# A two-layer diffusion backbone on one core: when the first map's row products are issued, and the order of the first input

## Chip, core and metric

The kernel runs on one NeuronCore of one Trainium2 chip. The metric is device time in microseconds (us) of one execution of the whole program. Engines are called by their names: TensorE (PE, with its weight loads as PEld), VectorE (DVE), ScalarE (ACT), GpSimd (POOL) and SyncE (SP), whose queue issues nearly all DMAs.

## What is computed

Two layers act on 384 tokens (one prompt of 128, one sample of 256) of width 1024 in float32. Cut to what matters:

```python
def _layer(x, cond, lp, mixer_fn):
    mod = silu(cond) @ lp['w_ada'] + lp['b_ada']          # 1024 -> 6 * 1024
    sh1, sc1, g1, sh2, sc2, g2 = split(mod, 6)
    y = mixer_fn(x * (1 + sc1) + sh1)                      # four mixers, four gates, w_o
    x = layernorm(ALPHA * x + g1 * y)
    f = square(relu((x * (1 + sc2) + sh2) @ lp['w_up'])) @ lp['w_down']
    return layernorm(ALPHA * x + g2 * f)
```

The mixer projects its input onto the queries, keys and values of four mixers (A latent attention, B two-way retention, C windowed attention, D grouped attention) and onto four gates, multiplies each mixer's output by a branch matrix and its gate, adds the four and applies `w_o`. There are two conditions (prompt and sample), so `mod` is two vectors of 6144 per layer. "The first map" is `w_ada`: it turns the condition into shifts, scales and gates.

## The kernel before

**Precision.** Each large product is made of three TensorE products of float32r halves: `mm3` (lines 119 to 122) multiplies high by high, high by low and low by high. A weight tile comes by DMA into one of six raw buffers of 128x1024 (`raw_load`, line 270). ScalarE casts it to its high half (line 281) and VectorE subtracts that for the low half (`split_low`, line 125). `Stream` (line 238) does this for all weights in the order of use: it loads four ahead and splits two ahead.

**The order of work.** Instructions are written in program order, and a scheduler then orders each engine's own by priority and readiness. Where the order matters the kernel pins it: `in_order` (line 156) keeps what is written inside it in written order on the engines named, `held` (line 145) keeps instructions behind given earlier ones of the same engine, and `keep` fixes single ones.

**The first input** (lines 473 to 561, layer 0 only). The shift and scale of the first modulation are needed before anything else. For each of eight groups k of 128 channels, `first_part(k)` makes the first map's product on TensorE: condition as weights, 16 products that leave four partial sums on four groups of partitions (line 330), copied out by ScalarE (line 333). `first_input(k)` transposes them (line 339), reduces the four partials on VectorE (line 341), adds the bias (line 343), adds one to the scale (line 495) and makes the modulated channels: ScalarE the high half (line 499), VectorE the full value (line 500) and the low half. `split_w(i)` splits the weights of two of the projection's column groups, `w_qa` (416 columns, mixer A) and `w_c0` (512 columns, mixer C). `chunk` (line 516) then adds one channel group's products into three banks (one per 128 tokens) of either. Four products with zeros stand ahead of it all (`WARM`, line 544). Only TensorE is kept in written order here.

**Attention.** The remaining projections come as `chunks` (line 1088), 256 columns at a time, through two PSUM banks (`psg`); the banks of mixers C and A are first evacuated by ScalarE (line 597, called in lines 1089 to 1095). Beside them runs `Pipe` (line 416): a list of tasks, each a list of stages; every `tick()` (line 464) starts one task and advances each live one by one stage. Layer 0 has 16 ticks in the projections (22 in layer 1) and then two per pair of gate products (`gates`, line 1109), eight per branch, in the order A, C, D, B. In `attend`, `scores` computes a score tile, its maximum, the exponentials and their sum, and scales the tile by the reciprocal (line 671); `turn`, a tick later, transposes it; `values` multiplies by the values. `at` is the pool of the attention; `t2` in it has ten tiles of 128x512. Behind the third branch it is closed and the pool `p2` opened.

**The rest of the first map.** Only 8 of its 48 parts are made on TensorE. The others are row products on VectorE: `ada_vector` (line 346) loads 128 transposed rows of `w_ada` into a raw buffer (line 357, three loads ahead on SP's queue) and multiplies them by a condition's row with a running sum (line 370), one instruction for each of the two conditions. The rows of SiLU of the conditions are made by `cond_rows` (line 226): a 1 MB load, four tanh on ScalarE (line 231), eight operations on VectorE (lines 232 and 233). Layer 0's attention makes 48 row products (its own first gate, and the modulation of its MLP), layer 1's makes 32; the MLPs make the rest. `tick` calls them by `TICK_OPS` a tick once the tick's number is over `TICKS_FROM`:

```python
            if ticks[0] > TICKS_FROM:          # 22
                for _ in range(TICK_OPS[l]):   # 3 in layer 0, 2 in layer 1
                    next(ada_v, None)
```

What is not done by then is drained where the attention's pool is closed (line 1159).

**Layer norms.** `out_product` (line 1274) ends with a written order over three blocks of tokens (lines 1316 to 1376): `sums`, `normalise` (ScalarE, two halves of 512, line 1219), `turn` (eight transposes in two banks, line 1227, with the modulation behind them), `high` (ScalarE's cast, line 1244) and `low` (VectorE's subtraction, line 125), mixed with the next product's parts (`following`, lines 610 and 614).

Of the kernel before, what the change touches and what calls it, by code (L numbers as in the profile page):

```python
# [16 lines left out]
P = 128  # L17
D = 1024
KT = D // P
NTOK = 384  # L20
# [20 lines left out]
TICK_OPS = (3, 2)  # L41
TICKS_FROM = 22
# [6 lines left out]
WARM = 4  # L49
# [44 lines left out]
def kernel(ctx, tc, a):  # L94
# [363 lines left out]
    for l in range(L):  # L458
        last = l == L - 1
        pipe = Pipe()  # L460
        ada_v = ada_vector(AV_GATES[l], lambda: t2("acc"))
        ticks = [0]

        def tick():
            pipe.step()
            ticks[0] += 1
            if ticks[0] > TICKS_FROM:
                for _ in range(TICK_OPS[l]):
                    next(ada_v, None)


        if l == 0:
            with tc.tile_pool(name="start", bufs=1, reuse_waits="tile") as st:
# [12 lines left out]
                def load_w(i):  # L486
                    raws[i] = [raw_load(a["w_qa"][0, i]), raw_load(a["w_c0"][i])]
# [16 lines left out]
                def split_w(i):  # L504
                    if i == 0:

                        wh, wl = (q[:, :2 * A_W] for q in o_pair())
                        for c in (slice(0, A_W), slice(A_W, 2 * A_W)):
                            nc.scalar.copy(wh[:, c], raws[i][0][:, c])
                            split_low(wl[:, c], raws[i][0][:, c], wh[:, c])  # L510
                        w_a.extend(by_k([(wh, wl)], 2))
                    else:
                        w_a.extend(by_k([split_raw(raws[i][0], o_pair)], 2))
                    w_c.extend(by_k([split_raw(raws[i][1], ring_hl)], 2))
# [26 lines left out]
                with in_order((mybir.EngineType.PE,)):  # L541
                    idle = bank(psm)
                    for _ in range(WARM):
                        mm(idle[:, 0:256], lhsT=zero[:, 0:P], rhs=zero, start=True, stop=True)
                    first_part(0)
                    first_input(0)
                    split_w(0)
                    banks_a = [bank(psa) for _ in range(3)]
                    banks_c = [bank(pso), bank(psg), bank(psg)]
                    for k in range(0, KT, 2):  # L550
# [8 lines left out]
                        else:  # L559
                            chunk(banks_c, w_c, 512, k + 1)  # L560
# [12 lines left out]
        if l == 0:  # L573
            smalls = small_loads(0)
            cond_rows(lambda: t2("acc"))
# [48 lines left out]
        def attend(i, q_of, k_of, v_of, scale, sink=None, mask=None):  # L624
            ob = {}

            def batch(g, us):
# [9 lines left out]
                def scores():  # L637
# [31 lines left out]
                    for i, (u, nb, c) in enumerate(segs):  # L669
                        for j in range(2):  # L670
                            nc.vector.tensor_scalar(out=p[:, j, c], in0=p[:, j, c], scalar1=su[:, i, j:j + 1],
                                                    scalar2=None, op0=ALU.mult)
# [421 lines left out]
        for t in range(3):  # L1094
            evac_to("a", 0)(t, banks_a[t], A_W)
        for key, c0, scale in chunks:
# [35 lines left out]
        p2 = None  # L1132
# [531 lines left out]
```

## Time and profile before

| what | us |
|---|---|
| median of 3 runs | 1293.54 (1293.39 to 1294.13) |
| the profiled execution | 1292.02 |
| its span, first to last instruction | 1290.3 |
| TensorE busy / weight loads busy | 1258.5 / 1139.1 |
| VectorE busy | 865.3 |
| ScalarE busy | 567.0 |
| GpSimd busy | 198.9 |

Busy time is the time in which an engine executes; register, branch, semaphore and DMA-issuing instructions don't count. Matmuls are pipelined and their ends are modelled, so the busy time of TensorE says where it waited, and not that it ran at its peak. PEclk is the clock granted to TensorE as a share of 2.4 GHz; 0.50 is 1.2 GHz. In the views, L125 is line 125 of the kernel, and "tile<-tile" are the names of what is written and read.

### The profile page before, as it was taken

Reading aid. Unit: us, or ns where it says so; the run is one execution under the profiler, and the core shown is the slowest. Engines: PE = TensorE matmul, PEld = TensorE weight load, DVE = VectorE, ACT = ScalarE, POOL = GpSimd, SP = SyncE. Lnnn points to the kernel's source line nnn. Section 1 sums busy time; section 2 is a strip of 40 time slices with the busy share of each in tenths; the row PEclk is TensorE's granted clock in tenths of the full one; section 3 lists DMA queues with packets and bytes.
Section 4 is the critical chain, followed back from the end, with each engine's and each line's share of the span. In section 5 each row is a group of like instructions: output and inputs, shape, how many; then the busy total and the mean of one; then the engine's idle time right before and its main releaser. Section 6 shows DMA issues by size and latency. Waiting matters only on the chain. (4 is left out here: it accounts for less than half of the span.)

```text
span 1290.3 us, 19064 instructions
## 1 busy us (share of the span) xinstructions
PE 1258.5 (98%) x7226; PEld 1139.1 (88%) x7226; DVE 865.3 (67%) x1572; ACT 567.0 (44%) x1014; POOL 198.9 (15%) x214
## 2 busy tenths in 40 slices
PE   8999999979999999999999999999999999999996
PEld 5789888979989999999998988899998999999995
DVE  4655887998668999543384678799465893333336
ACT  4564453323536444454455455333343644444441
POOL 0011200423214000000051210023221500000003
PEclk9999999999999999999999999999999999999999
DMA  9832244559434888554314223447644263334421
GB/s 368 304 111 93 86 147 135 176 196 328 165 127 172 279 271 270 189 164 145 130 51 146 72 93 115 150 148 235 240 148 163 89 228 125 131 131 149 164 80 50
DMA packets 64684, 211.66 MB, mean 164 GB/s; under 512 B 9232, under 2 KB 13264, under 8 KB 64464
## 3 DMA queue, kind: packets, MB, share of 16 engines
q1 hardware_dynamic: 61872, 201.49, 44.9%
q0 software_dynamic: 2432, 8.42, 1.9%
q8 instruction: 57, 0.93, 0.3%
q10 hardware_dynamic: 288, 0.52, 0.1%
q14 instruction: 35, 0.29, 0.1%
HBM read 206.28 MB, written 4.13 MB: 163 GB/s over the span
## 5 line engine op out<-in xcount | busy, mean ns | idle before, releaser
L125 DVE TENSOR_TENSOR wl<-raw,wh 128x1024 fp32r<-128x1024 f32 x250 | 320.8, 1289 | 295.9 <-ACT wh L281 295.6
L281 ACT CAST wh<-raw 128x1024 fp32r<-128x1024 f32 x250 | 261.6, 1050 | 467.1 <-PE bank L121 309.2
L122 PE MATMUL bank<-hTh,wl 128*128 128x384 f32 x1040 | 350.0, 337 | 5.7 <-DVE wl L125 5.7
L120 PE MATMUL bank<-hTh,wh 128*128 128x384 f32 x1040 | 351.8, 338 | 0.6 <-ACT tt L1116 0.6
L121 PE MATMUL bank<-hTl,wh 128*128 128x384 f32 x1040 | 349.0, 336 | 0.0
L122 PEld LDWEIGHTS bank<-hTh,wl 128*128 128x128 f32 x1040 | 195.7, 188 | 7.1 <-DVE wl L125 6.9
L120 PEld LDWEIGHTS bank<-hTh,wh 128*128 128x128 f32 x1040 | 195.9, 188 | 5.8 <-issue 2.3
L121 PEld LDWEIGHTS bank<-hTl,wh 128*128 128x128 f32 x1040 | 195.7, 188 | 2.7 <-issue 0.5
L121 PE MATMUL bank<-wl,uh 128*128 128x512 f32 x384 | 150.4, 392 | 0.0
L122 PE MATMUL bank<-wh,ul 128*128 128x512 f32 x384 | 150.3, 392 | 0.0
L120 PE MATMUL bank<-wh,uh 128*128 128x512 f32 x384 | 149.7, 390 | 0.0
L370 DVE CUSTOM_DVE_ANT_0 acc<-raw,csr,bT 128x1024 bf16<-128x1024 f32 x80 | 103.6, 1321 | 0.0
L370 DVE CUSTOM_DVE_ANT_0 acc<-lnc,csr,bT 128x1024 bf16<-128x1024 f32 x80 | 100.5, 1292 | 0.0
L1143 POOL TENSOR_TENSOR tt<-tt,tt 128x384 f32<-128x384 f32 x48 | 64.4, 1361 | 214.1 <-DVE tt L1142 213.0
L122 PEld LDWEIGHTS bank<-wh,ul 128*128 128x128 f32 x384 | 71.9, 188 | 15.4 <-DVE ul L125 0.4
L120 PEld LDWEIGHTS bank<-wh,uh 128*128 128x128 f32 x384 | 72.1, 188 | 13.8
L121 PEld LDWEIGHTS bank<-wl,uh 128*128 128x128 f32 x384 | 72.1, 188 | 13.9
L120 PE MATMUL bank<-wh,hTh 128*128 128x256 f32 x240 | 72.2, 301 | 2.3 <-ACT tmc L597 2.3
L121 PE MATMUL bank<-wl,hTh 128*128 128x256 f32 x240 | 69.4, 289 | 0.0
L122 PE MATMUL bank<-wh,hTl 128*128 128x256 f32 x240 | 68.7, 286 | 0.0
L120 PEld LDWEIGHTS bank<-wh,hTh 128*128 128x128 f32 x240 | 46.5, 194 | 5.4 <-ACT tmc L597 2.6
L663 ACT ACTIVATE p<-bank,neg 128x384 f32<-128x384 f32 (+1 forms) x72 | 35.9, 509 | 33.7 <-DVE neg L660 19.5
(263 smaller groups left out, 1758.1 us busy)
## 6 DMA issues: line engine op xcount, KB each, us to landing
raw<-in_w_g_dram SPq DMA_DIRECT2D x64, 512.0 KB, 3.6
raw<-in_w_d_dram SPq DMA_DIRECT2D x64, 512.0 KB, 3.5
raw<-in_w_u_dram SPq DMA_DIRECT2D x58, 512.0 KB, 4.0
raw<-in_w_av_dram SPq DMA_DIRECT2D x40, 512.0 KB, 3.3
lnc<-in_w_av_dram SPq DMA_DIRECT2D x40, 512.0 KB, 4.3
raw<-in_w_q_dram SPq DMA_DIRECT2D x28, 512.0 KB, 4.4
raw<-in_w_ada_dram SPq DMA_DIRECT2D x16, 512.0 KB, 8.5
raw<-in_w_b_dram SPq DMA_DIRECT2D x16, 512.0 KB, 4.0
```

The source lines that it names most:

```text
L120: mm(out, lhsT=a_hl[0], rhs=b_hl[0], start=start, stop=False)
L121: mm(out, lhsT=a_hl[0], rhs=b_hl[1], start=False, stop=False)
L122: mm(out, lhsT=a_hl[1], rhs=b_hl[0], start=False, stop=stop)
L125: nc.vector.tensor_tensor(out=low, in0=x, in1=high.bitcast(F32), op=ALU.subtract)
L281: nc.scalar.copy(wh, raw)
L370: nc.vector.tensor_tensor_reduce(out=alloc().bitcast(BF16), in0=w, in1=csr[:, c], scale=1.0, scalar=bT[:, l, u, b:b + 1], op0=ALU.mult, op ...
L663: nc.scalar.activation(p[:, j, c], ss[j][:, c], AF.Exp, bias=neg[:, i, j:j + 1], scale=scale, accum_out=su[:, i, j:j + 1])
L1143: nc.gpsimd.tensor_tensor(out=acc[c], in0=acc[c], in1=t_, op=ALU.add)
```

## The change

It does six things. The row products of the attention are issued by a table of rates per two ticks: in both layers one per tick from tick 4, one per two ticks from tick 14, two per tick from tick 29; once `p2` is open, one per tick, with outputs in its `v2` tiles. The loop that drains them moves from the closing of the attention's pool to the place before the layer norm's constants. The rows of the conditions are made behind the first evacuations instead of ahead of them. The first channel group has a function of its own, `first_channels`: two products with a 0/1 matrix in place of the transposes and the reduction, the tokens of the prompt first, the first weights cast and split between, all four engines in written order, with zero products of 64 columns (three behind the first map's product, six behind the sums); the first weight load is cut in two, and two weights of the stream are split before the last chunk. One of the two scalings of each score tile goes from VectorE to ScalarE. The third block's normalisation is cut so that a cast comes between its halves.

```diff
-TICK_OPS = (3, 2)
-TICKS_FROM = 22
+TICK_OPS = ((4, 2), (14, 1), (29, 4))
-WARM = 4
+WARM = (4, 3, 6)
...
-        ada_v = ada_vector(AV_GATES[l], lambda: t2("acc"))
+        p2 = None
+        ada_v = ada_vector(AV_GATES[l], lambda: (v2 if p2 else t2)("acc"))
...
-            if ticks[0] > TICKS_FROM:
-                for _ in range(TICK_OPS[l]):
-                    next(ada_v, None)
+            n = 2 if p2 else ([0] + [c for f, c in TICK_OPS if f <= ticks[0]])[-1]
+            for _ in range((n + ticks[0] % 2) // 2):
+                next(ada_v, None)
...
                 def load_w(i):
-                    raws[i] = [raw_load(a["w_qa"][0, i]), raw_load(a["w_c0"][i])]
+                    first = raw_tile(2 * A_W)
+                    n = 2 if i == 0 else 1
+                    for c in (slice(j * 2 * A_W // n, (j + 1) * 2 * A_W // n) for j in range(n)):
+                        nc.sync.dma_start(out=first[:, c], in_=a["w_qa"][0, i][:, c])
+                    raws[i] = [first, raw_load(a["w_c0"][i])]
...
+                def first_channels():
+                    (ah, al), (ch, cl) = tuple(q[:, :2 * A_W] for q in o_pair()), ring_hl()
+                    ra, rc = raws[0]
+                    a0, a1, c0, c1 = slice(0, A_W), slice(A_W, 2 * A_W), slice(0, 512), slice(512, 1024)
+                    _, xk, part = inputs[0]
+                    mod = modT[0][:, 0]
+                    sel = st.tile([P, 2], F32, name="sel")
+                    nc.vector.tensor_reduce(out=sel, in_=ident.rearrange("p (j c) -> p c j", j=4)[:, 0:2, :], axis=AX.X,
+                                            op=ALU.add)
+                    pt = bank(psm)
+                    for b in range(2):
+                        mm(pt[:, 2 * b:2 * b + 2], lhsT=part[:, b * P:(b + 1) * P], rhs=sel, start=True, stop=True)
+                    warm_up(WARM[2])
+                    nc.scalar.copy(ah[:, a0], ra[:, a0])
+                    nc.vector.tensor_tensor(out=mod, in0=pt[:, 0:4].rearrange("p (b c) -> p b c", b=2),
+                                            in1=bT[:, 0, 0].unsqueeze(2).to_broadcast([P, 2, 2]), op=ALU.add)
+                    nc.vector.tensor_scalar(out=ms[:, 0], in0=mod[:, 1], scalar1=1.0, scalar2=None, op0=ALU.add)
+                    hx = st.tile([P, NTOK], F32, tag="hx", name=nm("hx"), bufs=2)
+                    for cnd, cs in ((0, slice(0, P)), (1, slice(P, NTOK))):
+                        m, sh = ms[:, 0, cnd:cnd + 1], mod[:, 0, cnd:cnd + 1]
+                        nc.scalar.activation(hT[0][:, 0, cs], xk[:, cs], AF.Identity, bias=sh, scale=m)
+                        if cnd == 0:
+                            split_low(al[:, a0], ra[:, a0], ah[:, a0])
+                        nc.vector.tensor_scalar(out=hx[:, cs], in0=xk[:, cs], scalar1=m, scalar2=sh, op0=ALU.mult,
+                                                op1=ALU.add)
+                    split_low(hT[1][:, 0, :], hx, hT[0][:, 0, :])
+                    for h, lo, r, c in ((ch, cl, rc, c0), (ah, al, ra, a1), (ch, cl, rc, c1)):
+                        nc.scalar.copy(h[:, c], r[:, c])
+                        split_low(lo[:, c], r[:, c], h[:, c])
...
-                with in_order((mybir.EngineType.PE,)):
-                    idle = bank(psm)
-                    for _ in range(WARM):
-                        mm(idle[:, 0:256], lhsT=zero[:, 0:P], rhs=zero, start=True, stop=True)
+                idle = bank(psg)
+                def warm_up(n, cols=64):
+                    for _ in range(n):
+                        mm(idle[:, 0:cols], lhsT=zero[:, 0:P], rhs=zero[:, 0:cols], start=True, stop=True)
+                with in_order():
+                    warm_up(WARM[0], 256)
                     first_part(0)
-                    first_input(0)
-                    split_w(0)
+                    warm_up(WARM[1])
+                    first_channels()
+                with held(last_issued()), in_order((mybir.EngineType.PE,)):
...
                         else:
+                            for i in range(SPLITS_AHEAD):
+                                stream.split(i)
                             chunk(banks_c, w_c, 512, k + 1)
...
             smalls = small_loads(0)
-            cond_rows(lambda: t2("acc"))
...
-                        for j in range(2):
-                            nc.vector.tensor_scalar(out=p[:, j, c], in0=p[:, j, c], scalar1=su[:, i, j:j + 1],
-                                                    scalar2=None, op0=ALU.mult)
+                        nc.scalar.mul(p[:, 0, c], p[:, 0, c], su[:, i, 0:1])
+                        nc.vector.tensor_scalar(out=p[:, 1, c], in0=p[:, 1, c], scalar1=su[:, i, 1:2], scalar2=None,
+                                                op0=ALU.mult)
...
             evac_to("a", 0)(t, banks_a[t], A_W)
+        if l == 0:
+            cond_rows(lambda: t2("acc"))
         for key, c0, scale in chunks:
...
-                    for _ in ada_v:
-                        pass
                     at_ctx.__exit__(None, None, None)
...
-            def normalise():
-                for h in range(2):
+            def normalise(hs=(0, 1)):
+                for h in hs:
...
-                normalise[2]()
+                normalise[2]((0,))
                 high[1](1)
+                normalise[2]((1,))
...
+        for _ in ada_v:
+            pass
         c1 = norm_consts(0)
```

## Rows read from the trace of the kernel before

**Rows 1.** The page, part 1: busy us, share of the span, instructions.
```profile
PE 1258.5 (98%) x7226; PEld 1139.1 (88%) x7226; DVE 865.3 (67%) x1572; ACT 567.0 (44%) x1014; POOL 198.9 (15%) x214
```

**Rows 2.** Busy us by stretch: PE, PEld, DVE, ACT, POOL (counts), PEclk, DMA share, GB/s.
```profile
12.00:15.30 3.30, 3.30 (x21) 1.50 (x20) 0.72 (x1) 0.36 (x1) 0.00 (x0) 0.50 1.01 398
56.40:59.70 3.30, 3.30 (x17) 3.30 (x17) 3.25 (x10) 1.23 (x4) 1.11 (x2) 0.50 0.40 112
278.20:281.50 3.30, 3.30 (x12) 3.30 (x11) 3.30 (x5) 0.66 (x1) 0.00 (x0) 0.50 0.82 278
60.00:226.00 166.00, 165.58 (x1128) 145.65 (x1128) 116.50 (x291) 81.64 (x199) 20.21 (x31) 1.00 0.34 116
226.00:306.00 80.00, 71.29 (x407) 67.92 (x405) 80.00 (x162) 22.23 (x35) 27.33 (x19) 0.98 0.59 202
306.00:356.00 50.00, 49.59 (x281) 48.82 (x282) 33.48 (x41) 23.62 (x34) 16.05 (x14) 1.00 0.67 243
770.00:850.00 80.00, 79.18 (x543) 70.65 (x542) 64.24 (x154) 35.12 (x81) 5.92 (x6) 1.00 0.37 126
850.00:900.00 50.00, 49.05 (x287) 48.38 (x286) 49.52 (x93) 16.46 (x25) 15.85 (x12) 1.00 0.63 206
```

**Rows 3.** Waits of TensorE, whole span: us in total, times, longest us.
```profile
PE bank L122 <- DVE wl L125: 7.1, 5, 3.0
PE bank L120 <- ACT tmc L597: 2.3, 1, 2.3
...
PE bank L120 <- DVE atts L981: 1.3, 2, 0.8
PE bank L1227 <- DVE hTl L125: 1.3, 3, 0.6
```

**Rows 4.** Timeline, first input: start us, us, instruction, [idle before it and releaser].
```profile
10.12 0.45 PE L523 MATMUL bank<-o,hTh 128*128 128x416 f32 x1 [2.11 <-ACT o L509]
...
12.91 1.94 PE L330 MATMUL bank<-raw,cs 128*32 128x256 f32 x16
```

**Rows 5.** Timeline around the first evacuations.
```profile
49.02 3.88 ACT L281 CAST wh<-raw 128x1024 fp32r<-128x1024 f32 x4
...
52.80 2.19 ACT L231 ACTIVATE acc<-csr 128x512 f32<-128x512 f32 x4
...
54.89 1.53 ACT L597 COPY tmc<-bank 128x512 f32<-128x512 f32 x3
...
55.51 0.39 PE L120 MATMUL bank<-wh,hTh 128*128 128x256 f32 x1 [2.30 <-ACT tmc L597]
```

**Rows 6.** Timeline around the longest wait for a weight split.
```profile
275.38 1.22 DVE L125 TENSOR_TENSOR wl<-raw,wh 128x1024 fp32r<-128x1024 f32 x1
...
276.65 0.44 PE L122 MATMUL bank<-hTh,wl 128*128 128x384 f32 x1 [3.05 <-DVE wl L125]
```

**Rows 7.** Costliest group of VectorE from 226 to 311 us: count, busy us, mean ns.
```profile
L370 DVE CUSTOM_DVE_ANT_0 acc<-raw,csr,bT 128x1024 bf16<-128x1024 f32 x35 | 45.8, 1337 | 0.0
```

**Rows 8.** Busy time of line 370 alone from 770 to 850 us.
```profile
770.00:850.00 80.00, 19.38 (x31) 1.00 0.37 126
```

**Rows 9.** Group of TensorE's products with 64 float32 columns.
```profile
L1007 PE MATMUL bank<-tmb,atts 128*128 128x64 f32 x64 | 7.6, 271 | 0.0
```

**Rows 10.** Timeline, third block of the first layer norm.
```profile
391.60 1.52 ACT L1219 ACTIVATE z<-z,lnrs 128x512 f32<-128x512 f32 x2 [0.37 <-POOL lnrs L1215]
...
393.03 0.56 ACT L1244 CAST hTh<-bank 128x512 fp32r<-128x512 f32 x1
...
394.37 0.66 PE L1227 MATMUL bank<-ident,z 128*128 128x128 f32 x4 [0.58 <-DVE hTl L125]
```

**Rows 11.** Groups of the wide scalings on VectorE and of ScalarE's line 777.
```profile
L671 DVE TENSOR_SCALAR p<-p,su 128x384 f32<-128x384 f32 x48 | 17.9, 415 | 0.5
...
L777 ACT ACTIVATE qA<-bank,rsa 128x384 f32<-128x384 f32 x6 | 3.5, 583 | 4.4 <-PE bank L772 4.4
```

**Rows 12.** Waits of all engines, whole span: us in total, times, longest us.
```profile
ACT wh L281 <- DMA raw<-in_w_g_dram: 24.3, 8, 4.9
```

More of the change, by code (lines that the diff above doesn't have):

```diff
@@ L504, in split_w @@
                 def split_w(i):
[L505 to L513, printed above, removed]
@@ L514, in split_w @@
-                    w_c.extend(by_k([split_raw(raws[i][1], ring_hl)], 2))
+                    w_a.extend(by_k([split_raw(raws[i][0], o_pair)], 2))
+                    w_c.extend(by_k([split_raw(raws[i][1], ring_hl)], 2))
+                def first_channels():
[27 more added lines that the diff above has]
+                        split_low(lo[:, c], r[:, c], h[:, c])
+                    w_a.extend(by_k([(ah, al)], 2))
+                    w_c.extend(by_k([(ch, cl)], 2))
@@ L1130, in products, with v2 @@
                 done(c0 + i, ts_[i], b[:, :NTOK])
-        p2 = None
+        def v2(name):
+            return p2.tile([P, 512], F32, tag="v2", name=nm(name), bufs=7)
         def T2(name, dt):
@@ L1183, in norm_consts @@
             return gb + [lnc(a[n][l]) for n in names]
-        def v2(name):
-            return p2.tile([P, 512], F32, tag="v2", name=nm(name), bufs=7)
         def layer_norm(t, banks, xt, consts, mod, final):
```

## Prediction

> **What bounds the kernel now.** I began with the shares of the span: TensorE is busy 1258.5 us of 1290.3, 98% [rows 1]. No gain is to be had from the totals of another engine; there are some 32 us of idle TensorE to win, and whatever it spends at the lower clock. The second view, busy time by stretch, says where [rows 2]. From 226 to 306 us TensorE is idle 80.00 - 71.29 = 8.7 us while VectorE is busy 80.00 of 80, and three short stretches (from 12.0, 56.4 and 278.2 us) show PEclk 0.50, that is 1.2 GHz instead of 2.4. The third view, what TensorE waited for, names causes [rows 3]: 7.1 us for VectorE's low weight halves (line 125, read by line 122), 2.3 us for ScalarE's first evacuation (line 597), 1.3 us for a low half of the normalised rows (line 125, read by line 1227). Each low-clock stretch comes behind one of TensorE's longest idles: 2.11 us before 10.12 [rows 4], 2.30 us before 55.51 [rows 5], 3.05 us before 276.65 [rows 6].
>
> The big one is VectorE between 226 and 311 us [rows 7]: 35 of the first layer's 48 row products (line 370) run there, 45.8 us or 1.31 us each. VectorE is in order, so a weight split sits behind row products: the one that starts at 275.38 lets TensorE go at 276.65, after its 3.05 us [rows 6].
>
> **The change, part by part.** The sum is made against the profiled execution, 1292.0 us; its span of 1290.3 has 1.7 us around it. The median of the runs is 1293.5, 1.5 above it, and I add that back at the end.
>
> *Row products spread.* Before, layer 0 issues 3 per tick from tick 23: 48 in ticks 23 to 38. So the loop that drains the rest behind tick 40 finds nothing, and removing it is worth nothing by itself. After: 10 in ticks 4 to 13, 7 in ticks 14 to 28, 24 in ticks 29 to 40, and the last 7 one per tick behind the attention. In the crowded stretch 24 stand where 35 ran: 11 x 1.31 = 14.4 us of VectorE's 85 go, so it falls from all of the time to some 83%. The nearest stretch with that load is 770 to 850, VectorE 64.24 of 80 (80%), where TensorE idles 0.82 us [rows 2]. I leave 0.9 us of the 8.7: gain 7.8. The idle before the low clock at 278.2 goes with it; 3.4 us at half rate cost 1.7. Together **9.5** (ends: half of it, 4.7, if VectorE still comes late to half of the splits; 10.4 if nothing is left). The seven behind the attention, 9.2 us, fall into 306 to 356, where VectorE is busy 33.48 of 50 [rows 2]: hidden, and if that cover is gone the last branch's splits come late by up to 1.31 us each, as in the lower end.
>
> *What the early ones cost.* 17 row products per layer now come at ticks 4 to 28, where in layer 0 VectorE is busy 116.50 of 166 and TensorE idles 166 - 165.58 = 0.4 us [rows 2]. An attention step queued behind one is late by at most 1.31 us, and its reader is a tick away. Below: nothing. Above: the wait on line 981's scores, 0.8 us at its longest [rows 3], stood in 770 to 850, which holds 19.38 us of row products [rows 8]; 34 of them, 44.5 us, give 44.5/19.38 x 0.8 = 1.8. Between the two: **-1.0**. Each also takes one of ten scratch tiles for its output, which nothing in the trace prices; it goes into the same bounds. Their rows of weights come through SP's one queue and the six raw buffers, three loads ahead, from tick 4 on: that is a rival below.
>
> *Layer 1.* 32 products, 2 per tick from tick 23 before; after, 17 before tick 29 and 15 in ticks 29 to 36. TensorE idles 0.82 + 0.95 = 1.8 us from 770 to 900 [rows 2]; I take half, having no row for a smaller load there: **1.0** (0 to 1.8).
>
> *Condition rows behind the evacuations.* Four tanh, 2.19 us, stand on ScalarE between the casts, which end at 52.90, and the first evacuation at 54.89; TensorE waits 2.30 us until 55.51 [rows 5]. After the move the first evacuation (1.53/3 = 0.51) ends near 53.4, TensorE was done at 53.2: 0.3 is left, 2.0 gained, and with it the low clock at 56.4 (1.7): **3.7**, ends 2.0 and 4.0. The two early weight splits are among the four casts already, so I count nothing for them. The tanh then hold up the evacuations behind them by 2.2 us at most, which the two output banks cover. On SP the load of the condition rows moves behind five small cache loads; its users are later too, so nothing.
>
> *First input.* Two products with a 0/1 matrix replace two transposes and a reduction, so one VectorE step of three before the rows' affine goes; the cast of the first weight half, which TensorE waits for at 10.12, leaves that path [rows 4]; the first token block alone lets TensorE start. Against that stand nine 64-column warm-up products ahead of the first real one: two records each, 7.6/64 = 0.12 us per record by the nearest kind [rows 9], so 0.7 us behind the first map's product and 1.4 behind the sums. TensorE then starts near 9.8 instead of 10.12 and reaches the second input's product, without the waits inside the first chunk, about 1 us before 12.91. That one took 1.94 us at the low clock [rows 4]. Its data had landed by 12.91 but need not be far ahead, so I credit 0.9 and 0.5 of what the clock costs: **1.4**. Ends: -0.6 if the warm-ups outlast the chain and the clock drops anyway; 2.9 if start and clock are both won in full. Cutting the first weight load in two adds one issue to SP's queue, hidden behind loads that wait for bytes.
>
> *The third block's normalisation in halves.* The cast at 393.03 moves ahead of the second half of line 1219 (1.52/2 = 0.76 us) and so does the split that frees the bank for the transposes at 394.37, which wait 0.58 [rows 10]. That half itself then ends later, near 393.7, and is the next to be late. There are three such turns, 1.3 us in all [rows 3]: **1.0** (0 to 1.3).
>
> *Half of the softmax scaling to ScalarE.* 36 of 72 scalings leave VectorE at 0.415 us for the wide ones and go to ScalarE, where the nearest row, line 777 with the same width and a scale per row, takes 0.583 [rows 11]. ScalarE is busy 81.64 of 166 there [rows 2], and the transposes that read the result come a tick later: nothing, either way; if that cover is gone, the price is the rival below. The Trainium skill's page "ScalarE: Activation LUTs", section "Rules for kernel authors", speaks against the edit: it puts a plain multiplication on VectorE and not on ScalarE. The rows agree that the single step is dearer there; whether that costs time hangs on the cover.
>
> Sum: 9.5 - 1.0 + 1.0 + 3.7 + 1.4 + 1.0 = 15.6 us, so 1276.4 by the profiled execution and **1278** as the median.
>
> **The rivals.** *VectorE stays the bound of the crowded stretch.* 24 products at two per tick still meet the splits and the retention steps there. For it: 83% is an average. Against it: the stretch at 80% with 0.82 us of idle. Half of the 9.5 stays and the early ones cost their 1.8: gain 15.6 - 4.8 - 0.8 = 10.0, 1283.5.
>
> *Raw buffers run short: slower.* With one product per tick or per two, three of six raw buffers are held from tick 4 to 47 instead of for 16 ticks, and on SP a weight load queues behind a row load that waits for its buffer. ScalarE's casts waited 24.3 us, 8 times, for such loads [rows 12], while TensorE lost 8.7 us in the crowded stretch. Were that so at ticks 4 to 28 of both layers, 2 x 8.7 = 17.4 us would come on top of the sum: 1295.5, and up to 1299 with two low-clock stretches. It decides from 15.6/47 = 0.33 us on each of the 47 weights used in those ticks. Against it: only eight casts in the whole span waited so, and slower use also asks for fewer bytes per tick.
>
> *The scalings on ScalarE come late.* If each of the 24 wide ones lay on the path, 24 x 0.583 = 14.0 us eat the sum: 1292, no change. Each transpose would have to catch up with a step issued a tick ahead.
>
> *The start and the moved rows do not do what they say*: the order on an engine is chosen by a scheduler, and casts or tanh may again come first. Then 3.7 and 1.4 go: gain 10.5, 1283.
>
> **How the numbers follow.** Forecast as worked out 0.61; VectorE still the bound 0.18; start and rows unmoved 0.06; scalings late 0.06; raw buffers short 0.09. About 0.2% (2.6 us) is what a measurement of this kernel can tell from no change. Faster by more: 0.61 + 0.18 + 0.06 = 0.85; the same 0.06; slower 0.09. The lower end takes the upper bounds together: 10.4 + 1.8 + 4.0 + 2.9 + 1.3 = 20.4, 1273. The upper end takes in the rivals at 1283 and 1283.5 with their own bounds, 1286; the 0.15 of the last two cases stays outside.
>
> **What would show it.** Right: no wait of TensorE over 1 us on line 125's work between 220 and 310 us, VectorE below 90% there, PEclk 1.00 around 56 and 278 us, the first product behind the input stage within 0.5 us of its forerunner, and TensorE's idle down by 10 us or more. Wrong: casts that wait for raw loads between 65 and 220 us, scalings as the releaser of transposes, or a new wait on VectorE before tick 28. If the crowded stretch keeps over 4 us of idle, the first term was mis-sized.

## The result, and the profile after

The changed kernel takes **1278.02 us** (median of 4 runs, 1276.57 to 1279.75) against 1293.47 us for the kernel before beside it (4 runs, 1290.49 to 1294.13): ratio 0.9886, 95% interval 0.9863 to 0.9908. That is 15.45 us less by the medians, where 15.6 were forecast. The profiled execution took 1276.65 us, its span is 1274.5.

The page after, part 1 (busy us, share of the span, instructions), to be held against [rows 1]:

```profile
PE 1253.8 (98%) x7246; PEld 1137.6 (89%) x7246; DVE 854.1 (67%) x1537; ACT 583.5 (46%) x1051; POOL 211.2 (17%) x214
```

TensorE's idle time went from 1290.3 - 1258.5 = 31.8 us to 20.7, by 11.1. The other 4.7 us of the span's gain are busy time, about what the three stretches at 1.2 GHz cost (3.41 us each at half rate, 5.1 in all). Busy time by stretch after, with the columns of [rows 2]:

```profile
12.00:15.30 3.30, 2.69 (x23) 1.61 (x20) 0.73 (x3) 0.37 (x1) 0.00 (x0) 1.00 1.03 401
56.40:59.70 3.30, 3.30 (x30) 3.30 (x29) 3.09 (x9) 1.94 (x7) 0.36 (x1) 1.00 0.89 330
278.20:281.50 3.30, 3.30 (x21) 3.30 (x20) 3.30 (x7) 1.55 (x2) 1.36 (x2) 1.00 0.85 281
60.00:226.00 166.00, 163.18 (x1107) 143.00 (x1106) 119.64 (x284) 89.98 (x213) 29.78 (x32) 1.00 0.36 121
226.00:306.00 80.00, 78.51 (x468) 77.69 (x467) 74.27 (x144) 24.48 (x36) 29.02 (x24) 1.00 0.60 205
306.00:356.00 50.00, 49.96 (x264) 46.48 (x263) 37.81 (x49) 23.45 (x34) 10.88 (x8) 1.00 0.73 261
770.00:850.00 80.00, 79.40 (x512) 72.78 (x511) 54.39 (x137) 32.71 (x70) 5.87 (x6) 1.00 0.33 112
850.00:900.00 50.00, 49.06 (x283) 48.45 (x282) 35.85 (x51) 17.78 (x25) 17.25 (x15) 1.00 0.71 256
```

All three stretches at 1.2 GHz are gone (PEclk 1.00 in the first three lines); in both kernels the only other such stretch lies behind the last product. Between 226 and 306 us TensorE idles 1.5 us instead of 8.7. VectorE, however, is still busy there for 74.27 of 80 us, 93%. The waits of TensorE over the whole span, with the columns of [rows 3]:

```profile
PE bank L1086 <- DVE oB L1078: 1.8, 2, 1.5
PE bank L718 <- ACT p L707: 1.5, 3, 0.8
PE bank L330 <- DMA raw<-in_w_ada_dram: 1.4, 3, 0.6
...
PE bank L122 <- DVE wl L125: 0.6, 1, 0.6
...
PE bank L120 <- ACT tmc L634: 0.2, 1, 0.2
```

The 7.1 us on low weight halves became 0.6, the 2.3 us on the first evacuation 0.2, and the wait of the transposes on the normalised rows' low half is no longer listed. Three small waits have moved to the top: the retention's normalisation on VectorE (line 1078; 0.9 us before), the score tiles scaled on ScalarE (line 707; 0.5 us before, on VectorE), and the loads of the first map's weights (0.4 us before).

Where the time came from is best read from instructions that both programs share. Each row gives an instruction's start in the two profiled executions; the last column, the worth of the stretch that ends there, is worked out from the differences.

| start of (us) | before | after | difference | of that stretch |
|---|---|---|---|---|
| last of the first map's products | 45.07 | 43.92 | -1.15 | first input -1.15 |
| first projection product behind the first evacuation | 55.51 | 52.28 | -3.23 | wait on the evacuation -2.08 |
| evacuation of the first gate product | 144.44 | 140.45 | -3.99 | low clock at 56.4, 11 of the 17 early row products: -0.76 |
| evacuation of the 17th gate product | 261.62 | 257.66 | -3.96 | the other 6 early row products: +0.03 |
| first turn of layer norm 1, layer 0 | 381.09 | 367.17 | -13.92 | crowded stretch **-9.96** |
| the same turn, layer 1 | 1004.98 | 989.81 | -15.17 | two turns -0.90, layer 1's attention -0.37 |
| last product | 1279.65 | 1263.97 | -15.67 | third turn -0.49 |

### The profile page after: what moved, and what is told of

Its sections match the earlier page's. It is cut to its first block, busy times and chain, and to the rows that moved or that the text cites. A ratio compares the mean times of both kernels' runs of the same rounds, so it can differ in the third digit from the quotient of the medians.

```text
span 1274.5 us, 19089 instructions
## 1 busy us (share of the span) xinstructions
PE 1253.8 (98%) x7246; PEld 1137.6 (89%) x7246; DVE 854.1 (67%) x1537; ACT 583.5 (46%) x1051; POOL 211.2 (17%) x214
## 5 line engine op out<-in xcount | busy, mean ns | idle before, releaser
L125 DVE TENSOR_TENSOR wl<-raw,wh 128x1024 fp32r<-128x1024 f32 (+1 forms) x251 | 317.6, 1270 | 299.4 <-ACT wh L281 298.8
L370 DVE CUSTOM_DVE_ANT_0 acc<-lnc,csr,bT 128x1024 bf16<-128x1024 f32 x80 | 100.5, 1293 | 0.0
```

The costliest lines, as they stand in the source:

```text
L125: nc.vector.tensor_tensor(out=low, in0=x, in1=high.bitcast(F32), op=ALU.subtract)
L370: nc.vector.tensor_tensor_reduce(out=alloc().bitcast(BF16), in0=w, in1=csr[:, c], scale=1.0, scalar=bT[:, l, u, b:b + 1], op0=ALU.mult, op ...
```

## The experiments

Twelve kernels. Ratios are to the kernel before, run beside them. At a median near 1293, 0.001 is 1.3 us. "Marks" are starts of shared instructions as in the table above. A "..." stands where lines of a diff or the end of a line are left out.

**The spread undone (e1).** The changed kernel with the old rates: six per two ticks (four in layer 1) from tick 23, and a drain of the rest.

```diff
-TICK_OPS = ((4, 2), (14, 1), (29, 4))
+TICK_OPS = (((23, 6),), ((23, 4),))
...
-            n = 2 if p2 else ([0] + [c for f, c in TICK_OPS if f <= ticks[0]])[-1]
+            n = 2 if p2 else ([0] + [c for f, c in TICK_OPS[l] if f <= ticks[0]])[-1]
```

> The changed kernel with the old rates alone: 3 row products per tick from tick 23 in layer 0, 2 in layer 1. My sum gave the spread 9.5 - 1.0 + 1.0 = 9.5 us; by the marks of the two profiles it gave 10.0 in the crowded stretch, 0.4 in layer 1 and took 1.0 early. Every theory of how expects 9 to 10 us more than the changed kernel: 1287 to 1288, that is 0.995 to 0.996 of the kernel before. If it stays at 1278, the spread is not what moved.

Measured: 1286.07 us, ratio 0.9954 (0.9937 to 0.9971). Some 6 us of the gain stay, 9 go. The crowded stretch by engine, and the longest waits of TensorE in it:

```profile
226.00:306.00 80.00, 70.86 (x404) 68.15 (x404) 80.00 (x158) 22.26 (x34) 30.61 (x21) 0.98 0.63 200
PE bank L122 <- DVE wl L125: 7.1, 4, 3.0
```

This is the stretch of the kernel before again, with its 7.1 us on line 125 and its low clock (now at 298.3 us). So the spread is worth 8 to 9 us in the changed kernel by the medians, and 10.6 by the marks from the end of the first input to the last product; the other parts make some 5 to 6.

**VectorE's time or the rows' loads (e2).** The kernel of e1 with each attention row product on 512 of its 1024 columns. This leaves out half of each such product; the loads and buffers stay as they are.

```diff
-                nc.vector.tensor_tensor_reduce(out=alloc().bitcast(BF16), in0=w, in1=csr[:, c], scale=1.0,
+                nc.vector.tensor_tensor_reduce(out=alloc().bitcast(BF16) if raw else alloc().bitcast(BF16)[:, :512], in0=w if raw else w[:, :512],
+                                               in1=csr[:, c] if raw else csr[:, c, :512], scale=1.0,
```

(`raw` is set for the row products of the MLPs alone, which stay whole.)

> As the old rates, but each of the attention's row products multiplies 512 of its 1024 columns (the sums are of half a row); loads, buffers and order stay. VectorE's work in the stretch falls by 35 x 0.65 = 23 us. If VectorE's time is what the splits waited for, nearly all of the loss goes: within 1.5 us of the changed kernel, 1277 to 1279.5. If the row loads held the raw buffers and SP's queue, at least half of the loss stays: 1282 to 1287.

Measured: 1274.03 us, ratio 0.9847 (0.9829 to 0.9865). The crowded stretch:

```profile
226.00:306.00 80.00, 79.62 (x474) 78.37 (x475) 70.20 (x173) 27.01 (x41) 29.93 (x25) 1.00 0.79 273
```

TensorE's idle there is 0.4 us with the old rates and the loads unchanged. What bounded the stretch was the time of the row products on VectorE, not their transfers. The time lies 3 us below the range that was expected, though full clock came late in this execution (last section): by the marks the crowded stretch is 2.0 us shorter than in the changed kernel, and the stretch from the end of the second turn to layer 1's first turn 2.5. So some 4 us of the changed kernel still hang on VectorE's row products there, although TensorE's idle shows 1.5 in the first of the two.

**Three per tick from tick 29 (e3).** Early products as in the change; the crowd gets three a tick instead of two.

```diff
-TICK_OPS = ((4, 2), (14, 1), (29, 4))
+TICK_OPS = ((4, 2), (14, 1), (29, 6))
```

> The changed kernel with 3 row products per tick from tick 29 instead of 2: the same 24 in 8 ticks, ended at tick 36. If the total of VectorE's work in the stretch decides, the backlog is shorter lived than before the change and some of the loss returns, 2 to 5 us: 1280 to 1283. If it is the number of products ahead of one split (3 against 2), the loss returns nearly whole: 1285 to 1288.

Measured: 1288.24 us, ratio 0.9962 (0.9948 to 0.9977). The stretch and its longest wait:

```profile
226.00:306.00 80.00, 73.38 (x412) 70.54 (x411) 75.90 (x149) 22.45 (x35) 25.71 (x20) 0.96 0.59 188
PE bank L122 <- DVE wl L125: 5.4, 4, 3.0
```

VectorE's total (75.90) is hardly above that of the changed kernel (74.27), yet TensorE idles 6.6 us instead of 1.5, and 1.2 GHz is back for 6.83 us from 270.3. The share of VectorE's busy time doesn't tell the two cases apart. The time is that of the second expectation, the number ahead of one split; e4 tries it.

**Four in one tick, none in the next (e4).** The same mean rate as the change, but in bursts: a split may stand behind four row products, more than e3 ever puts into a tick.

```diff
-            for _ in range((n + ticks[0] % 2) // 2):
+            for _ in range((n if n < 4 else 0 if ticks[0] % 2 else 8) // 2 if n != 1 else ticks[0] % 2):
```

> The changed kernel with 4 row products at each even tick from 30 and none at the odd ones: the same rate, 5.2 us in one piece. If the total decides, nothing or up to 1 us: 1278 to 1279. If the number ahead of one split decides, 5 us or more are lost: 1283 to 1290.

Measured: 1276.36 us, ratio 0.9876 (0.9855 to 0.9898).

```profile
226.00:306.00 80.00, 78.63 (x469) 77.93 (x468) 75.06 (x144) 25.29 (x38) 27.78 (x24) 1.00 0.62 207
```

No loss. So it isn't the number of row products ahead of one split that decides. The reading that fits e3, e4 and the change together is a backlog: at three per tick VectorE falls behind, until the splits come after their readers; four in one tick are worked off in the next. The traces bear it out. VectorE's backlog is the time from the end of ScalarE's cast of a weight tile to the start of its split on VectorE. A cast and its split where it is longest, in e3, and then in the changed kernel:

```profile
255.36 1.05 ACT L281 CAST wh<-raw 128x1024 fp32r<-128x1024 f32 x1 [3.32 <-DMA raw<-in_w_g_dram]
269.99 1.22 DVE L125 TENSOR_TENSOR wl<-raw,wh 128x1024 fp32r<-128x1024 f32 x1
...
253.28 1.05 ACT L281 CAST wh<-raw 128x1024 fp32r<-128x1024 f32 x1 [0.64 <-PE bank L121]
265.13 1.22 DVE L125 TENSOR_TENSOR wl<-raw,wh 128x1024 fp32r<-128x1024 f32 x1
```

The split is 13.6 us late in e3 and 10.8 in the change; at its longest it is 12.2 in the kernel before, 12.3 in e1, 8.0 in e4 and 8.7 in e2. Of the fourteen kernels' traces, TensorE waits on line 125 between 226 and 310 us in the four with 12.2 us or more (before, e1, e3, e12), and in none of the ten with 10.8 or less.

**Both scalings back on VectorE (e5).**

```diff
-                        nc.scalar.mul(p[:, 0, c], p[:, 0, c], su[:, i, 0:1])
-                        nc.vector.tensor_scalar(out=p[:, 1, c], in0=p[:, 1, c], scalar1=su[:, i, 1:2], ...)
+                        for j in range(2):
+                            nc.vector.tensor_scalar(out=p[:, j, c], in0=p[:, j, c], scalar1=su[:, i, j:j + 1], ...)
```

> The changed kernel with both scalings of a score tile on VectorE again. My sum put nothing on this edit: within 0.5 us of the changed kernel. The changed profile shows transposes that wait 1.5 us, 3 times, for ScalarE's scaling: if that is a cost of the edit, it is 1 to 1.5 us faster without it. If the edit pays by the room it makes on VectorE (36 x 0.415 = 15 us over both layers), waits on VectorE take their place and it is 1 to 3 us slower.

Measured: 1280.56 us, ratio 0.9914 (0.9898 to 0.9931). By the marks, counted from the end of the first input (which came 0.6 us earlier in this execution), the last product comes 2.6 us later than in the changed kernel: 1.1 of it by the 17th gate, 0.6 in the crowded stretch, 0.9 in layer 1's attention. The edit that was costed at nothing is worth some 2 us in this place; the interval overlaps that of the changed kernel, so the size rests on the marks.

**Condition rows in front again (e6).**

```diff
+            cond_rows(lambda: t2("acc"))
...
-        if l == 0:
-            cond_rows(lambda: t2("acc"))
```

> The changed kernel with the rows of the conditions made ahead of the first evacuations again. My sum: 3.7 us slower, 2.0 of it the wait at the first product of the projections and 1.7 the low clock that followed. If the low clock does not come back, 2.0 us slower.

Measured: 1282.11 us, ratio 0.9924 (0.9902 to 0.9946). The longest wait of TensorE:

```profile
PE bank L120 <- ACT tmc L635: 3.2, 1, 3.2
```

The wait is back, longer than before, and so is the low clock, at 55.64 us. By the marks from the end of the first input on, it costs 2.9 us at the first product of the projections, 3.4 at the first gate and 3.7 at the end. So up to the first gate the move gains 0.5 us beyond the wait, not the 1.7 that was counted for the low clock.

**The normalisation in one piece (e7).**

```diff
-                normalise[2]((0,))
+                normalise[2]()
                 high[1](1)
-                normalise[2]((1,))
```

> The changed kernel with the third block's normalisation in one piece. My sum: 1.0 us slower; by the marks of the two profiles 0.50 + 0.40 + 0.49 = 1.4 at the three turns. If the turns gained for another reason, nothing.

Measured: 1277.34 us, ratio 0.9886 (0.9872 to 0.9901): no difference in the medians. The marks show it all the same: across the three turns this kernel gains 0.01, 0.01 and -0.01 us on the kernel before, where the changed one gains 0.50, 0.40 and 0.49. The start of this execution was 0.5 us earlier and layer 1's attention, with the same code, 1.2 us shorter; a part worth 1.4 us is below what these medians resolve.

**The first channel group as before (e8).** The old order at the start: transposes, a reduction, all tokens at once, the weights behind.

```diff
-                    n = 2 if i == 0 else 1
+                    n = 1
...
-                with in_order():
+                with in_order((mybir.EngineType.PE,)):
                     warm_up(WARM[0], 256)
                     first_part(0)
-                    warm_up(WARM[1])
-                    first_channels()
-                with held(last_issued()), in_order((mybir.EngineType.PE,)):
+                    first_input(0)
+                    first_halves()
```

(`first_halves` splits the first weights as the kernel before did.)

> The changed kernel with the first channel group made as before, the first weight load in one piece and no zero products of 64 columns. My sum: 1.4 us slower; by the marks 1.2 at the last of the first map's products. If the low clock from 12 us comes back, its second product takes 0.9 us more; if it stays away, the two products with the 0/1 matrix and the order are worth 0.5 us or less.

Measured: 1279.62 us, ratio 0.9903 (0.9889 to 0.9918). The waits of TensorE that answer to it:

```profile
PE bank L562 <- ACT o L516: 2.1, 1, 2.1
PE bank L120 <- DVE tt L1189: 2.0, 1, 2.0
```

The first line is the wait of [rows 4], back with a low clock at 11.0 us; the last of the first map's products starts at 45.18 us, 1.26 later than in the changed kernel. The second line lies between 340 and 385 us and has nothing to do with the input: the scheduler's order moved far from the edit. So the price of this part is read at the mark, not from the median.

**The spread alone (e9).** The kernel before with the new rates, the late products in `v2` tiles and the drain at the new place.

```diff
-TICK_OPS = (3, 2)
+TICK_OPS = ((4, 2), (14, 1), (29, 4))
...
-                    for _ in ada_v:
-                        pass
                     at_ctx.__exit__(None, None, None)
```

> The kernel before with the spread of the row products alone (the new rates, the late ones behind the attention). Theory (most of the gain is the spread: VectorE's backlog in the crowded stretch): 9 to 10 us less than the kernel before, a time near 1283, TensorE's idle from 226 to 306 us below 3 us, no low clock near 278 us, the low clock at 12 and 56 us kept. Rival (the spread works only together with the scalings that leave VectorE, whose undoing alone cost 2 to 2.6 us): a gain of 5 us or less, 1288 or more, waits on the weights' low halves left in that stretch.

Measured: 1286.94 us, ratio 0.9945 (0.9932 to 0.9957), a gain of 7.1: between the two expectations. Its stretches:

```profile
60.00:226.00 166.00, 165.26 (x1122) 145.53 (x1122) 121.89 (x302) 81.95 (x199) 30.70 (x33) 0.99 0.38 122
226.00:306.00 80.00, 78.29 (x465) 76.55 (x464) 73.63 (x149) 25.20 (x38) 25.73 (x21) 1.00 0.56 176
```

The crowd gains all that it gains in the changed kernel: 9.7 us by the marks (9.96 there). But 0.65 us go before it and 2.07 us in layer 1's attention, most of them between 750 and 790 us: 9.7 - 0.65 - 2.07 = 7.0. In the changed kernel these two stretches lose nothing. The size of the second loss is uncertain: e5, which has the same rates and scalings, loses 0.55 us there.

**Other rates (e10).** One per tick from 4 to 28, then three in two ticks.

```diff
-TICK_OPS = ((4, 2), (14, 1), (29, 4))
+TICK_OPS = ((4, 2), (14, 2), (29, 3))
```

> The changed kernel with other rates: one row product per tick from tick 4 to 28, then three in two ticks (18 in the crowd, 43 of 48 by tick 40, the rest behind). Theory (the crowd is already under its bound; TensorE idles 1.5 us there and 2.8 us ahead of it): at most 1.5 us gained in the crowd, 0.5 to 1 us lost ahead of it, so 1277 to 1279, the same as the changed kernel. Rival (VectorE, still busy 93% of the crowd, goes on bounding TensorE in ways that its idle does not show): 2 us or more gained, 1276 or less.

Measured: 1276.73 us, ratio 0.9875 (0.9858 to 0.9892): not told apart from the changed kernel.

```profile
226.00:306.00 80.00, 78.77 (x466) 77.66 (x465) 72.55 (x148) 25.25 (x37) 24.46 (x22) 1.00 0.65 217
```

By the marks 1.9 us are lost between the first and the 17th gate, 0.03 in the changed kernel. The crowd and what follows it to the first turn give back 1.4 of that; from the first product behind the evacuations to the first turn, 1.0 us is lost in all. Here the early products have a price.

**Both scalings on ScalarE (e11).**

```diff
-                        nc.vector.tensor_scalar(out=p[:, 1, c], in0=p[:, 1, c], scalar1=su[:, i, 1:2], ...)
+                        nc.scalar.mul(p[:, 1, c], p[:, 1, c], su[:, i, 1:2])
```

> The changed kernel with both scalings of a score tile on ScalarE. Theory (what the moved scaling gained came from shorter queues on VectorE, and ScalarE has room): 0.5 to 2 us less than the changed kernel, about 1277, VectorE some 13 us less busy. Rival (ScalarE becomes the late one: its two scalings of 0.6 us each stand behind weight casts of 1.05 us): TensorE's waits on the scaled tile, 1.5 us in three waits in the changed kernel, grow to 4 us or more, 1280 or more.

Measured: 1276.64 us, ratio 0.9867 (0.9852 to 0.9882). The interval overlaps that of the changed kernel, and the difference of the marks, 0.5 us at the last product, is there whole at the end of the first input. So nothing more is gained by the second scaling, and nothing lost: the waits on the scaled tile stay at 1.6 us, not 4.

```profile
PE bank L717 <- ACT p L707: 1.6, 3, 0.8
```

**The scaling alone (e12).** The kernel before with the edit of the scaling and nothing else (the diff of e5, read the other way).

> The kernel before with the one scaling of each score tile on ScalarE, and nothing else of the change. Theory (the scaling pays by making room on VectorE for the early row products: the spread alone lost 0.7 us before the crowd and 2.1 us in layer 1's projections, the changed kernel neither): nothing to be had without the spread, within 1 us of the kernel before, its first score-heavy ticks (before 226 us) and layer 1's projections moved by less than 0.7 us. Rival (shorter steps of the attention pay by themselves): 2 us or more less, in these two stretches.

Measured: 1292.91 us, ratio 0.9999 (0.9991 to 1.0008): nothing, within 1.2 us. In the profiled execution 1.5 us are gained around 56 us, where this execution has no low clock (below); from there to the 17th gate the marks move by 0.3 us, and layer 1's attention gains 0.5. So the 2 us of e5 aren't the scaling's own: it pays only beside the spread. That it does so by making room in VectorE's queue for the row products is the likely reason; no run shows that step by itself.

## Why the prediction was right, and where it was not

**Row products spread: 9.5 forecast, 9.96 by the marks of the stretch.** The named mechanism held: e2 shows that VectorE's time was the bound, e1 and e3 bring the loss back. But a step of the term failed: "it falls from all of the time to some 83%", and with it the sign "VectorE below 90% there". VectorE is busy 93% in the stretch, and 100% from 260 to 300 us. The step took a window of time for a fixed set of work. Its 24 are the row products of ticks 29 to 40, its 35 all that ran in a window, five of them from ticks 27 and 28; by ticks the old rate had 30 there, so 6 x 1.31 = 7.9 us go and not 14.4. As counted, 24 row products run between 238 and 298 us; but that is 60 us and not 80, and what stood behind it moved in. VectorE's groups from 226 to 306 us, with the columns of [rows 7], first before (35 row products there, as in [rows 7]):

```profile
L125 DVE TENSOR_TENSOR wl<-raw,wh 128x1024 fp32r<-128x1024 f32 x13 | 18.1, 1396 | 0.0
L1142 DVE SCALAR_TENSOR_TENSOR tt<-tt,bank 128x384 f32<-128x384 f32 x10 | 5.2, 543 | 0.0
```

and after:

```profile
L370 DVE CUSTOM_DVE_ANT_0 acc<-raw,csr,bT 128x1024 bf16<-128x1024 f32 x26 | 34.7, 1360 | 0.0
L125 DVE TENSOR_TENSOR wl<-raw,wh 128x1024 fp32r<-128x1024 f32 x16 | 22.4, 1400 | 3.0 <-ACT wh L281 3.0
L1182 DVE SCALAR_TENSOR_TENSOR tt<-tt,bank 128x384 f32<-128x384 f32 x14 | 7.2, 545 | 0.0
```

Three splits and four products of a gate with its branch more are done in the same 80 us, and two of the seven late row products stand in it as well. The size of the term came out right although the rule behind it was wrong: TensorE's idle isn't read off VectorE's share (e3 and the change differ by 2% of the window in share and by 5.1 us in idle), but off whether VectorE's backlog outgrows what the splits are ahead of their readers (12.2 us and more against 10.8, as shown with e4). The idle of the split's line shows the sign of it: VectorE now waits 3.0 us there for ScalarE's casts, so at times it is ahead of them, where before it never was. The rival "VectorE stays the bound" had the load right and the consequence wrong. The 9.96 are of one execution: the same stretch gains 8.0 to 10.2 us in e5 to e9 and e11, which have the same rates.

**Early row products: -1.0 forecast, nothing shown in the changed kernel**, -0.65 in layer 0 with the scalings left on VectorE (e9), and 1.0 more, net, at twice the rate in ticks 14 to 28 (e10). The table's +0.03 covers only 6 of the 17; the other 11 run before the first gate, where the table shows a gain. The test is e1, which has none of them: from the first product behind the evacuations to the 17th gate it takes 205.96 us, the changed kernel 205.38. The step also had the load wrong. The kernel before had 14 row products of its own between 60 and 226 us (the first at 171), and the changed one has 17: VectorE's busy time there rises from 116.50 to 119.64 us only, with half of the scalings gone from it. The cost lies in the bounds given; what the step missed besides is its cover, which is the next point.

**The scaling: "nothing, either way".** This step failed by a link between two parts. Alone the edit is worth nothing (e12), as forecast; beside the spread it is worth 2 to 2.6 us (e5; e9's losses, 0.65 + 2.07, are of that size). The steps on ScalarE are indeed dearer, the wide ones 0.62 us against 0.415 [rows 11], by this view of ScalarE's groups with shapes kept apart:

```profile
L707 ACT ACTIVATE p<-p,su 128x384 f32<-128x384 f32 x24 | 14.9, 623 | 4.9 <-DVE su L705 4.8
L707 ACT ACTIVATE p<-p,su 128x128 f32<-128x128 f32 x12 | 4.8, 398 | 0.0
```

The rule of the Trainium skill's page "ScalarE: Activation LUTs", section "Rules for kernel authors", names the dearer engine rightly; by the runs, the dearer step costs nothing here that the marks of e11 show, and which engine has the longer queue seems to decide.

**Layer 1: 1.0 forecast, 0.4 by the marks, and none of it shown to be the spread's.** TensorE's idle from 770 to 900 us is 0.6 + 0.9 = 1.5 us, where it was 1.8. But from the end of the second turn to layer 1's first, where the kernel before takes 339.86 us and the changed one 339.48, e6, e7 and e8 with the same code there take 338.78, 338.27 and 340.04, and e1 with the old rates 338.98: undoing the spread loses nothing. The scaling alone gains 0.5 (e12). With the scalings left on VectorE the spread loses 0.55 (e5) to 2.07 (e9). So this term failed: the idle that it meant to win hardly moved, and the gain of 0.4 is less than kernels with the same code differ by. What TensorE spends in e9 isn't seen as a wait; it stays open.

**Condition rows: 3.7 forecast, 2.8 by the table up to the first gate, 3.4 there in e6.** The wait was right (2.0 forecast, 2.08 in the table, 2.9 in e6). The clock's half was mis-sized: 1.7 forecast, 0.76 in the table, 0.5 in e6. The low clock itself is worth 1.4 to 1.5 us (e12, below). But from the evacuation to the first gate TensorE idles 1.60 us where it idled 0.11, and 0.7 to 1.0 us of the clock's worth are missing. The early row products aren't the cause: e1, without them, gains no more in that stretch (0.62). By e6, which differs in the place of the rows alone, the moved rows have a price there of 1.0 us (an estimate, 1.4 less the 0.45 that it shows), so the step "which the two output banks cover" seems to have failed; which wait carries the price is open.

**First input: 1.4 forecast, 1.15 to 1.26.** Its parts (the 0/1 matrix, the order, the zero products, the cut load) were undone together in e8 and aren't told apart. The start as worked out is met: the first product behind the input starts at 9.73 us, 9.8 forecast. The timeline of TensorE after, with the columns of [rows 4]:

```profile
9.73 0.43 PE L554 MATMUL bank<-o,hTh 128*128 128x416 f32 x1
...
11.61 0.63 PE L330 MATMUL bank<-raw,cs 128*32 128x256 f32 x4
12.84 1.06 PE L330 MATMUL bank<-raw,cs 128*32 128x256 f32 x12 [0.61 <-DMA raw<-in_w_ada_dram]
```

The second group's product now comes before the last of its weights: a wait of 0.61 us has taken the place of the low clock, as the prediction's doubt on that transfer had it. **Normalisation: 1.0 forecast, 1.4 (e7)**, 0.4 to 0.5 per turn.

**Rivals.** Raw buffers short: refuted, and its sign did not appear: between 65 and 220 us no cast waits for a load, before or after. Over the whole span the casts do wait more for loads, to be held against [rows 12]:

```profile
ACT wh L281 <- DMA raw<-in_w_g_dram: 31.0, 13, 6.4
```

These waits lie between 260 and 310 us and between 845 and 865, and in the whole span TensorE waits on line 125 but once, 0.6 us. Scalings late: the sign appeared, 1.5 us in three waits, and not 24 times 0.583. So did a new wait on VectorE before tick 28, 0.44 us at 69.72. TensorE's idle from 60 to 226 us did rise from 0.4 to 2.8 us, with those waits among its causes (the longest, 0.76 us, at 132.73). From the first gate to the 17th it shows as next to nothing, 117.21 us against 117.18. But most of the rise, 1.5 us, lies before the first gate, the stretch in which 0.7 to 1.0 us of the low clock's gain are missing, so there it is at least in part time lost.

By the table the sum reads 9.96 (spread) + 0.4 (layer 1) + 2.8 (condition rows) + 1.15 (first input) + 1.4 (normalisation) = 15.7 us; the medians give 15.45, and the interval of the ratio 11.9 to 17.7. That the forecast of 15.6 hit so closely is in part luck: the spread, the normalisation and the uncharged early products came out 1.9 us better than forecast, layer 1, the condition rows and the first input 1.8 us worse.

## What to carry to other kernels

Background work on an in-order engine is placed by its rate against the time the engine has left in each step of the schedule: two row products a tick fit here and three did not, at nearly the same busy share, and bursts of four did no harm as long as the mean fitted. The delay between a tile's cast and its split shows this where the busy share doesn't. Before work is moved into a quiet stretch, its engine's queue there needs room too; a second edit that looks worthless alone can be what makes that room, so such pairs are tried singly and together. Parts worth under some 2 us are read from the starts of shared instructions in the trace, since medians of a few runs hide them; and a mark needs its own measure of noise, since kernels with the same code in a stretch differed there by up to 1.8 us.

## What was unexpected of the hardware

**When full clock begins varies between executions.** In the changed kernel's profiled execution 2.4 GHz was granted from 4.5 us on; in that of e9 the input's products still ran at the lower clock and the first stretch granted 1.00 began at 17.6 us, in that of e2 at 16.7. In e9 the product behind the input's wait of 2.11 us took 0.71 us (0.45 in [rows 4]), those behind it 0.55 (0.35 after), and the second input's product began at 16.00 us instead of 12.91:

```profile
12.26 0.71 PE L523 MATMUL bank<-o,hTh 128*128 128x416 f32 x1 [2.11 <-ACT o L509]
...
13.44 0.55 PE L523 MATMUL bank<-o,hTh 128*128 128x416 f32 x1
...
16.00 1.81 PE L329 MATMUL bank<-raw,cs 128*32 128x256 f32 x16
```

The Trainium skill's page "TensorE: Matmul & The Clock Gate" (part 1, "What you observe") states that the point of the rise varies by some 500 ns from run to run. That it varies, these traces bear out, but not the size: the changed kernel and e2, written alike up to there, lie 12.2 us apart, and the measurement decides. Such a start moves a whole execution by some 3 to 4 us; that it also makes the scatter of the medians' runs (1276.6 to 1279.8 for one kernel) is likely and was not shown.

**The same idle doesn't always bring the low clock.** In e12 TensorE waits 2.30 us for the first evacuation, as in [rows 5], and goes on at full clock: the products from 56.35 us on take 0.28 us each, and no stretch at 1.2 GHz follows until 277.2 us. In the kernel before, the same products take 0.42 us from 56.34 on. The timeline of e12:

```profile
56.00 0.39 PE L120 MATMUL bank<-wh,hTh 128*128 128x256 f32 x1 [2.30 <-ACT tmc L597]
56.23 0.29 PE L121 MATMUL bank<-wl,hTh 128*128 128x256 f32 x1
56.35 0.28 PE L122 MATMUL bank<-wh,hTl 128*128 128x256 f32 x1
```

The low clock in that place was worth 1.4 to 1.5 us by the marks, near the 1.7 that the prediction counted for it. What decides whether it comes is open: the same idle of 2.30 us was followed by it in one execution and not in the other.
